# Operands of the first FFN moved by 192 bytes, table loads moved to another queue and later, three more constant matmuls

## The chip, the cores and the metric

The kernel runs on one core of a Trainium2 chip. The metric is device time in microseconds (us) of one execution; the median of three runs of the kernel before is 2201.35 us (2201.22 to 2201.47). The change is judged by that time alone.

## The reference, cut to what matters

One layer of a decoder trunk over T = 272 positions (16 learned tokens ahead of 256 tokens), width 2048, all in float32:

```
h += 1/2 * SwiGLU_1(RMSNorm(h))              # first FFN, 2048 -> 5632 -> 2048, 272 positions
u  = RMSNorm(h);  z = u @ W_in               # mix: sparse attention and a gated short convolution
h += W_out(sigmoid(ga) * y_attn + sigmoid(gc) * y_conv)
h += 1/2 * SwiGLU_2(RMSNorm(h))              # second FFN, 256 positions
return h without the first 16 positions
```

`SwiGLU(x) = (silu(x @ w_gate) * (x @ w_up)) @ w_down`. All weights together are some 390 MB and each is read from HBM once.

## The kernel before, in words

**Numbers in two parts.** Each float32 value is split into a high part (`hi`, type float32r) and the rest (`lo`). A product is made of three matmuls, whi*xhi, whi*xlo and wlo*xhi (`mac`, lines 263 to 265), or, where the two parts of x lie in one 512-column operand, of two (`paired`, lines 277 and 278: whi against xhi and xlo together, wlo against xhi).

**The stream of weights.** `Stream` (line 53) takes the weights in program order. Each load of 1 MB is one DMA on SyncE's queue (SP, line 93) into one of three `raw` buffers. A load is split in pieces of 8 blocks of 128x128 by ScalarE (`whi`, line 108) and VectorE (`wlo`, line 109), three pieces ahead of use. TensorE takes block after block; each is the stationary operand of two or three matmuls, and the columns of the activations stream past it. `st.later(fn, lag)` and `st.early(fn, lag)` put other work behind or ahead of the split of a coming piece; `tables` is put at lag 16.

**Where operands lie.** `act` holds the normalised input of a stage: for each of 16 blocks of rows a row of `PITCH` = 320 float32 for hi and one for lo. `mid` holds the FFN's inner values in the same form. `LINE` is 64 float32, 256 bytes, so a row is five lines; in the built program both tiles begin on a multiple of 256 bytes. The first FFN writes and reads columns 0 to 271 of a row (`FIRST` = 0). The mix and the second FFN use columns 48 to 319 (`LATER` = 48, that is 192 bytes behind the start of a line), so that the 256 tokens proper begin on a line. In the second FFN a row of `mid` is 256 columns, all used.

**The stages.** `start_tiles` runs the first four products of the first FFN side by side while loads still arrive (PSUM tiles `start`). Then come gate and up products (`pg`, `pu`, 16 blocks deep), the down products (`pd`, 22 blocks deep), twice over; then the mix, whose first five products (`pkv`, three matmuls a block, 272 columns, `act` from column 48) have the first FFN's very shape; then the second FFN with paired matmuls. The norm's factor is applied behind the product, so that a stage can begin before the sum of squares is known; one small matmul (`norm`, line 348) adds that sum up across partitions.

**The beginning.** TensorE first multiplies a constant tile by itself nine times (`WARM`, line 259) while nothing has arrived. The first loads of weights and of `h` alternate on SP's queue; a first block of `h` and 16 columns of `small` go out on ScalarE's. The other tables (the rest of `small`, `ident`, `rope`, `cbias`) go out on GpSimd's queue (POOL, lines 236 to 239); GpSimd has nothing to wait for, so they leave at once although their place in the program is lag 16. Their first readers: the second gain in `small` at the end of the first FFN, the rest in the mix.

Of the kernel before, what the change touches and what calls it, by code (L numbers as in the profile page):

```python
# [17 lines left out]
KD = D // P  # L18
# [4 lines left out]
META = 16  # L23
# [23 lines left out]
RAW_BUFS = 3  # L47
SPLIT_BUFS = 4
AHEAD = 3
WARM = 9  # L50

LINE = 64
PITCH = 5 * LINE
FIRST, LATER = 0, LINE - META
SUB = 1024
RAW = 2048

# [95 lines left out]
def tile_decoder_layer(  # L155
# [22 lines left out]
    nc = tc.nc  # L178
# [7 lines left out]
    st = Stream(nc, raw_pool, split_pool)  # L186
# [30 lines left out]
    small = const.tile([P, SMALL], F32, name="small")  # L217
    rope = const.tile([P, 3, ROPE], F32, name="rope")
    cbias = const.tile([P, 2, T], F32, name="cbias")
    ident = const.tile([P, P], F32, name="ident")  # L220
# [12 lines left out]
    st.load(3, [load_h(1, 2), load_h(2, 4), load_h(4, 8), load_h(8, 12), load_h(12, 16)])  # L233

    def tables():
        nc.gpsimd.dma_start(small[:, KD:], small_in[:, KD:])
        nc.gpsimd.dma_start(ident, ident_in)
        nc.gpsimd.dma_start(rope, rope_in)
        nc.gpsimd.dma_start(cbias, cbias_in)

    st.later(tables, 16)

    o = 3 * KD
    gains = [small[:, i * KD : (i + 1) * KD] for i in range(3)]
# [5 lines left out]
    def mm_tile(name="mm"):  # L250
        return psum.tile([P, 512], F32, name=name, tag="mm")
# [5 lines left out]
    warm = mm_tile("warm")  # L257
    for _ in range(WARM):
        nc.tensor.matmul(warm[:, :P], ones, ones, start=True, stop=True)
# [7 lines left out]
    def fmajor(ps, xhi, xlo, n):  # L267

        for k in range(n):
            whi, wlo = st.next()  # L270
            mac(ps, whi, wlo, xhi(k), xlo(k), k == 0, k == n - 1)

    def paired(ps, x, n):

        for k in range(n):
            whi, wlo = st.next()
            nc.tensor.matmul(ps.rearrange("p (a t) -> p a t", a=2), whi, x(k), start=k == 0, stop=False)  # L277
            nc.tensor.matmul(ps[:, :SEQ], wlo, x(k)[:, 0, :], start=False, stop=k == n - 1)  # L278

    def joined(out, ps):  # L280
        u = tmp.tile([P, T], F32, name="u", tag="sq")[:, :SEQ]
        nc.scalar.activation(u, ps[:, SEQ:], AF.Copy)
        nc.vector.tensor_add(out, ps[:, :SEQ], u)
# [10 lines left out]
    def split_into(hi, lo, src):  # L294
        nc.scalar.activation(hi, src, AF.Copy)
        nc.vector.tensor_sub(lo, src, hi.bitcast(F32))

    def parts(at):

        return (lambda k, c0=0, c1=T: act[:, k, 0, at + c0 : at + c1]), (  # L300
            lambda k, c0=0, c1=T: act[:, k, 1, at + c0 : at + c1]
        )

    def next_act(d, gain, c0, at):

        x = h[:, d, c0:]
        g = gain[:, d : d + 1]
        hi, lo = (f(d, c0) for f in parts(at))
        nc.scalar.activation(hi, x, AF.Copy, scale=g)
        nc.vector.scalar_tensor_tensor(lo, x, g, hi.bitcast(F32), op0=ALU.mult, op1=ALU.subtract)  # L310
# [28 lines left out]
    def norm(c0, lag, ps, columns=False):  # L339

        box = {}

        def total():
            nc.vector.tensor_add(ssq[0][:, c0:], ssq[0][:, c0:], ssq[1][:, c0:])

        def across():
            row = ps[:, :T] if not columns else ps[:, 0, :T]
            nc.tensor.matmul(row[:, c0:], ones, ssq[0][:, c0:], start=True, stop=True)
            box[0] = rsqrt(R[:, c0:], row[:, c0:], (P, T - c0), 1.0 / D)
            if columns:  # L350
                for j, t0 in enumerate((0, META, META + P)):
                    nc.tensor.matmul(
                        ps[:, 1, 2 * j : 2 * j + 2], ssq[0][:, t0 : t0 + P], ones[:, :2], start=True, stop=True
                    )

        def inverse():
            box[0][1]()
            if columns:
                nc.vector.tensor_mul(R2, R, R)
                for fn in rsqrt(rcol, ps[:, 1, :6], (P, 6), 1.0 / D):  # L360
                    fn()

        st.later(total, lag)
        st.early(across, lag + 1)
        st.later(lambda: box[0][0](), lag + 1)
        st.later(inverse, lag + 2)

    def start_tiles(n, xhi, xlo):

        two = [aux_tile(f"start{i}") for i in range(2)]  # L370
        four = [two[i // 2][:, i % 2, :] for i in range(4)]
        for k in range(KD):
            for ps in four:
                whi, wlo = st.next()
                mac(ps[:, :n], whi, wlo, xhi(k), xlo(k), k == 0, k == KD - 1)
        return four

    def ffn(c0, at, done, wait, starting):
        n = T - c0
        a_hi, a_lo = parts(at)  # L380
        pitch = PITCH if n > SEQ else SEQ
        with tc.tile_pool(name=f"ffn{c0}", bufs=2, reuse_waits="tile") as fp:
            mid = fp.tile([P, FHALF, 2, pitch], F32R, name="mid", bufs=1)
            i_hi, i_lo = mid[:, :, 0, :n], mid[:, :, 1, :n]
            xhi, xlo = (lambda k: a_hi(k, c0)), (lambda k: a_lo(k, c0))
            pairs = n == SEQ

            def up(ps):
                if pairs:
                    paired(ps, lambda k: act[:, k, :, at + c0 : at + T], KD)  # L390
                else:
                    fmajor(ps[:, :n], xhi, xlo, KD)

            def down(ps, last):
                if pairs and not last:
                    paired(ps, lambda k: mid[:, k, :, :], FHALF)
                else:
                    fmajor(ps[:, :n], lambda k: i_hi[:, k, :], lambda k: i_lo[:, k, :], FHALF)

            def normed(out, ps):  # L400
                if pairs:
                    joined(out, ps)
                    nc.vector.tensor_mul(out, out, R[:, c0:])
                else:
                    nc.vector.tensor_mul(out, ps[:, :n], R[:, c0:])

            def gate(pg, box):
                box["t"] = fp.tile([P, n], F32, name="t")
                normed(box["t"], pg)

            def silu(box):
                box["s"] = fp.tile([P, n], F32, name="s")
                nc.scalar.activation(box["s"], box["t"], AF.Silu)

            def times(pu, box):
                box["v"] = fp.tile([P, n], F32, name="v")
                normed(box["v"], pu)
                nc.vector.tensor_mul(box["v"], box["v"], box["s"])

            norm(c0, wait, mm_tile("norm"))  # L420
            least = st.at + wait + 1
            for c in range(2):
                for f in range(FHALF):
                    box = {}
                    side = int(starting and c == 0 and f < 2)
                    if side:
                        if f == 0:
                            four = start_tiles(n, xhi, xlo)
                        pg, pu = four[2 * f : 2 * f + 2]
                    else:  # L430
                        pg, pu = mm_tile("pg"), mm_tile("pu")
                        up(pg)
                    st.later(lambda pg=pg, box=box: gate(pg, box), 1, least)
                    st.later(lambda box=box: silu(box), 2, least + 1)
                    if not side:
                        up(pu)
                    st.later(lambda pu=pu, box=box: times(pu, box), 1 + side, least + 1)
                    st.later(lambda f=f, box=box: split_into(i_hi[:, f, :], i_lo[:, f, :], box["v"]), 2 + side, least + 2)
                for d in range(KD):
                    pd = mm_tile("pd")  # L440
                    last = d == KD - 1 and c == 1
                    down(pd, last)
                    st.later(lambda d=d, pd=pd, last=last: add_to(h[:, d, c0:], pd, 0.5, pairs and not last))
                    if c == 1:
                        done(d)
            if not starting:
                st.flush()
# [3 lines left out]

    for u in range(AHEAD + 1):
        for d in (u,) if u < 2 else (2 * u - 2, 2 * u - 1):
            next_act(d, gains[0], 0, FIRST)
        st.split(u + 1)
    for u in range(AHEAD + 1, KD // 2 + 1):
        st.early(lambda u=u: [next_act(d, gains[0], 0, FIRST) for d in (2 * u - 2, 2 * u - 1)], u - AHEAD + 1)
    for d in range(KD):
        st.later(lambda d=d: square(d, 0), 4 + d * 7 // KD)

    def done1(d):
        st.later(lambda: (next_act(d, gains[1], 0, LATER), square(d, 0)), 2)

    ffn(0, FIRST, done1, 10, True)


    with ExitStack() as mix:
# [578 lines left out]
```

## Time and profile before

| | us |
|---|---|
| median of three runs | 2201.35 |
| the profiled execution, its own time | 2201.42 |
| its span, first to last instruction | 2199.3 |
| first FFN | from 7.26 to 806.08 of the span |
| mix | to 1461.5 |
| second FFN | to the end |

The profiled execution's time is 2.1 us above its span (2201.42 against 2199.3), and 0.07 us above the median. How to read the rows below: times in rows of the timeline are from the span's start; a row of the timeline gives start, duration, engine, line, operation and operands, and in brackets how long the engine had been idle and what ended that. The durations of matmuls overlap, since they are pipelined; the pace of TensorE is the distance from one start to the next, which is why first and last rows of a stretch are shown with the count between. In the table of stretches the count of matmuls takes in the two that reach over from the stretch ahead. "PEclk" is the granted clock of TensorE as a share of full speed, 2.4 GHz.

### The profile page before, as it was taken

Reading aid. Unit: us, or ns where it says so; the run is one execution under the profiler, and the core shown is the slowest. Engines: PE = TensorE matmul, PEld = TensorE weight load, DVE = VectorE, ACT = ScalarE, POOL = GpSimd, SP = SyncE. Lnnn points to the kernel's source line nnn. Section 1 sums busy time; section 2 is a strip of 40 time slices with the busy share of each in tenths; the row PEclk is TensorE's granted clock in tenths of the full one; section 3 lists DMA queues with packets and bytes.
Section 4 is the critical chain, followed back from the end, with each engine's and each line's share of the span. In section 5 each row is a group of like instructions: output and inputs, shape, how many; then the busy total and the mean of one; then the engine's idle time right before and its main releaser. Section 6 shows DMA issues by size and latency. Waiting matters only on the chain.

```text
span 2199.3 us, 34921 instructions
## 1 busy us (share of the span) xinstructions
PE 2188.4 (100%) x14548; PEld 2014.9 (92%) x14548; DVE 1318.3 (60%) x1848; ACT 1015.9 (46%) x1460; POOL 17.7 (1%) x30
## 2 busy tenths in 40 slices
PE   9999999999999999999999999999999999999999
PEld 8999999999999998798988888888888888888888
DVE  7555544455555555786566677676666556666654
ACT  6434433343444445564454455554444444444443
POOL 0000000000000000000000000000000000000000
PEclk9999999999999999999999999999999999999999
DMA  6544555444445445444455555545555555555553
GB/s 243 192 173 173 175 179 179 177 173 173 173 174 178 179 153 191 157 151 152 166 181 190 192 173 191 191 174 192 191 190 191 192 191 192 189 188 188 189 206 132
DMA packets 56510, 397.89 MB, mean 181 GB/s; under 512 B 6560, under 2 KB 7328, under 8 KB 8864
## 3 DMA queue, kind: packets, MB, share of 16 engines
q1 hardware_dynamic: 55296, 393.36, 50.7%
q8 instruction: 114, 1.87, 0.3%
q0 software_dynamic: 768, 2.16, 0.3%
q14 instruction: 44, 0.36, 0.0%
q10 hardware_dynamic: 288, 0.15, 0.0%
HBM read 393.54 MB, written 2.10 MB: 180 GB/s over the span
## 4 chain that ended last, share of the span: by engine, by line
PE 97%; DVE 1%; ACT 1%; DMA 1%; issue 0%; DVEq 0%; ACTq 0%
PE pu L277 7%; PE pg L277 7%; PE pd L277 7%; PE pgt L277 5%; PE pd L263 4%; PE pd L265 4%; PE pd L264 4%; PE pu L265 4%; PE pu L264 4%; PE pu L263 4%; PE pg L265 4%; PE pg L264 4%; PE pg L263 4%; PE pu L278 4%; PE pg L278 4%; PE pd L278 4%
## 5 line engine op out<-in xcount | busy, mean ns | idle before, releaser
L109 DVE TENSOR_TENSOR wlo<-raw,whi 128x1024 fp32r<-128x1024 f32 (+1 forms) x747 | 913.3, 1223 | 807.2 <-ACT whi L108 806.5
L108 ACT ACTIVATE whi<-raw 128x1024 fp32r<-128x1024 f32 (+1 forms) x747 | 789.0, 1057 | 999.3 <-issue 159.2
L277 PE MATMUL pg<-act,whi 128*128 128x512 f32 x704 | 246.3, 394 | 0.4 <-DVE act L310 0.4
L277 PE MATMUL pu<-act,whi 128*128 128x512 f32 x704 | 246.2, 394 | 0.0
L277 PE MATMUL pd<-mid,whi 128*128 128x512 f32 x682 | 236.5, 394 | 0.0
L265 PE MATMUL pd<-mid,wlo 128*128 128x272 f32 (+1 forms) x726 | 208.6, 287 | 0.0
L264 PE MATMUL pd<-mid,whi 128*128 128x272 f32 (+1 forms) x726 | 208.6, 287 | 0.0
L263 PE MATMUL pd<-mid,whi 128*128 128x272 f32 (+1 forms) x726 | 208.6, 287 | 0.0
L278 PE MATMUL pg<-act,wlo 128*128 128x256 f32 x704 | 195.1, 277 | 0.0
L278 PE MATMUL pu<-act,wlo 128*128 128x256 f32 x704 | 195.0, 277 | 0.0
L263 PE MATMUL pg<-act,whi 128*128 128x272 f32 x672 | 193.4, 288 | 0.0
L265 PE MATMUL pg<-act,wlo 128*128 128x272 f32 x672 | 193.3, 288 | 0.0
L264 PE MATMUL pg<-act,whi 128*128 128x272 f32 x672 | 193.2, 288 | 0.0
L263 PE MATMUL pu<-act,whi 128*128 128x272 f32 x672 | 193.2, 288 | 0.0
L264 PE MATMUL pu<-act,whi 128*128 128x272 f32 x672 | 193.2, 288 | 0.0
L265 PE MATMUL pu<-act,wlo 128*128 128x272 f32 x672 | 193.2, 288 | 0.0
L278 PE MATMUL pd<-mid,wlo 128*128 128x256 f32 x682 | 188.9, 277 | 0.0
L277 PE MATMUL pgt<-act,whi 128*128 128x512 f32 x512 | 182.2, 398 | 0.0
L277 PEld LDWEIGHTS pg<-act,whi 128*128 128x128 f32 x704 | 132.0, 188 | 31.4 <-DVE act L310 0.7
L277 PEld LDWEIGHTS pu<-act,whi 128*128 128x128 f32 x704 | 132.0, 188 | 30.7
L277 PEld LDWEIGHTS pd<-mid,whi 128*128 128x128 f32 x682 | 127.9, 188 | 29.7
L278 PE MATMUL pgt<-act,wlo 128*128 128x256 f32 x512 | 143.8, 281 | 0.0
(218 smaller groups left out, 4041.9 us busy)
## 6 DMA issues: line engine op xcount, KB each, us to landing
raw<-in_wgu_dram SPq DMA_DIRECT2D x175, 1024.0 KB, 4.8
raw<-in_wd_dram SPq DMA_DIRECT2D x88, 1024.0 KB, 4.8
raw<-in_wcv_dram SPq DMA_DIRECT2D x24, 1024.0 KB, 4.7
raw<-in_wgc_dram SPq DMA_DIRECT2D x24, 1024.0 KB, 4.7
raw<-in_wga_dram SPq DMA_DIRECT2D x24, 1024.0 KB, 4.7
raw<-in_wo_dram SPq DMA_DIRECT2D x16, 1024.0 KB, 4.7
raw<-in_wqi_dram SPq DMA_DIRECT2D x8, 1024.0 KB, 4.8
raw<-in_wq_dram SPq DMA_DIRECT2D x8, 1024.0 KB, 4.7
```

Source lines behind the costliest of these rows:

```text
L108: nc.scalar.activation(hi[:, :n], raw, AF.Copy)
L109: nc.vector.tensor_sub(lo[:, :n], raw, hi[:, :n].bitcast(F32))
L263: nc.tensor.matmul(ps, whi, xhi, start=first, stop=False)
L264: nc.tensor.matmul(ps, whi, xlo, start=False, stop=False)
L265: nc.tensor.matmul(ps, wlo, xhi, start=False, stop=last)
L277: nc.tensor.matmul(ps.rearrange("p (a t) -> p a t", a=2), whi, x(k), start=k == 0, stop=False)
L278: nc.tensor.matmul(ps[:, :SEQ], wlo, x(k)[:, 0, :], start=False, stop=k == n - 1)
```

## The change

Three edits. `WARM` goes from 9 to 12. The four table loads are issued by SP and not by GpSimd. The first FFN's operands in `act` lie from column 48 of a row (`LATER`), not from 0, and those in `mid` too (`pitch - n` = 320 - 272 = 48 in the first FFN, 256 - 256 = 0 in the second, which is as before).

```diff
-WARM = 9
+WARM = 12
...
-FIRST, LATER = 0, LINE - META
+LATER = LINE - META
...
     def tables():
-        nc.gpsimd.dma_start(small[:, KD:], small_in[:, KD:])
-        nc.gpsimd.dma_start(ident, ident_in)
-        nc.gpsimd.dma_start(rope, rope_in)
-        nc.gpsimd.dma_start(cbias, cbias_in)
+        nc.sync.dma_start(small[:, KD:], small_in[:, KD:])
+        nc.sync.dma_start(ident, ident_in)
+        nc.sync.dma_start(rope, rope_in)
+        nc.sync.dma_start(cbias, cbias_in)
...
-            i_hi, i_lo = mid[:, :, 0, :n], mid[:, :, 1, :n]
+            i_hi, i_lo = (mid[:, :, i, pitch - n :] for i in range(2))
...
-            next_act(d, gains[0], 0, FIRST)
+            next_act(d, gains[0], 0, LATER)
...
-        st.early(lambda u=u: [next_act(d, gains[0], 0, FIRST) for d in (2 * u - 2, 2 * u - 1)], u - AHEAD + 1)
+        st.early(lambda u=u: [next_act(d, gains[0], 0, LATER) for d in (2 * u - 2, 2 * u - 1)], u - AHEAD + 1)
...
-    ffn(0, FIRST, done1, 10, True)
+    ffn(0, LATER, done1, 10, True)
```

On SP's queue, whose loads the stream of weights lives on, the beginning of the program reads as follows (a 128x2048 load of `raw` is 1 MB, x9 means nine in a row):

```order
 L93 DMA raw<-in_wgu_dram 128x2048
 L231 DMA h<-in_h_dram 128x1088
-L93 DMA raw<-in_wgu_dram 128x2048 x41
+L93 DMA raw<-in_wgu_dram 128x2048 x9
+L236 DMA small<-in_small_dram 128x320
+L237 DMA ident<-in_ident_dram 128x128
+L238 DMA rope<-in_rope_dram 128x144
+L239 DMA cbias<-in_cbias_dram 128x544
+L93 DMA raw<-in_wgu_dram 128x2048 x32
 L93 DMA raw<-in_wd_dram 128x2048 x22
 L93 DMA raw<-in_wgu_dram 128x2048 x44
```

The four table loads now stand behind the twelfth load of 1 MB of weights, in the midst of the first FFN's gate and up products.

On GpSimd's queue the same place, right behind the constant tile `ones` that the first matmuls read:

```order
 L1041 UNCONDITIONAL_BRANCH
 L225 MEMSET ones 128x128
-L236 DMA small<-in_small_dram 128x320
-L237 DMA ident<-in_ident_dram 128x128
-L238 DMA rope<-in_rope_dram 128x144
-L239 DMA cbias<-in_cbias_dram 128x544
 L570 MEMSET hss 128x16
 L850 ISA
```

GpSimd has no load left at the beginning. On TensorE, VectorE and ScalarE the order of instructions is the same as before but for the three added matmuls.

## Rows read from the trace of the kernel before

**Rows 1.** The page: busy us of each engine, and chain by engine.

```profile
PE 2188.4 (100%) x14548; PEld 2014.9 (92%) x14548; DVE 1318.3 (60%) x1848; ACT 1015.9 (46%) x1460; POOL 17.7 (1%) x30
...
PE 97%; DVE 1%; ACT 1%; DMA 1%; issue 0%; DVEq 0%; ACTq 0%
```

**Rows 2.** Stretches, TensorE: length, busy us (matmuls), clock, DMA share, GB/s.

```profile
42.06:276.67 234.61, 234.61 (x1874) 1.00 0.49 174
276.67:409.00 132.33, 132.33 (x1058) 1.00 0.49 176
409.00:673.67 264.67, 264.67 (x2114) 1.00 0.49 175
673.67:806.08 132.41, 132.41 (x1058) 1.00 0.49 173
1099.70:1461.50 361.80, 361.80 (x2050) 1.00 0.53 186
1468.60:2073.40 604.80, 604.80 (x3491) 1.00 0.54 189
```

**Rows 3.** Timeline of TensorE: end of the first FFN, beginning of the mix.

```profile
794.06 0.28 PE L263 MATMUL pd<-mid,whi 128*128 128x272 f32 x1
...
806.08 0.29 PE L263 MATMUL pkv<-act,whi 128*128 128x272 f32 x1
...
811.88 0.29 PE L265 MATMUL pkv<-act,wlo 128*128 128x272 f32 x1
...
826.00 0.29 PE L263 MATMUL pkv<-act,whi 128*128 128x272 f32 x1
...
836.85 0.29 PE L264 MATMUL pkv<-act,whi 128*128 128x272 f32 x1
836.98 0.28 PE L265 MATMUL pkv<-act,wlo 128*128 128x272 f32 x1
```

**Rows 4.** Timeline of TensorE and ScalarE: the four products run side by side.

```profile
18.14 0.29 PE L263 MATMUL start<-act,whi 128*128 128x272 f32 x1
...
34.74 0.29 PE L265 MATMUL start<-act,wlo 128*128 128x272 f32 x1
...
34.94 1.06 ACT L108 ACTIVATE whi<-raw 128x1024 fp32r<-128x1024 f32 x1 [1.20 <-PE start L264]
```

**Rows 5.** Timeline of the first 17 us: TensorE's waits and a ScalarE split.

```profile
7.26 0.43 PE L263 MATMUL start<-act,whi 128*128 128x272 f32 x1 [2.54 <-ACT whi L108]
...
13.03 0.39 PE L265 MATMUL start<-act,wlo 128*128 128x272 f32 x1 [0.47 <-DVE wlo L109]
...
14.40 1.06 ACT L108 ACTIVATE whi<-raw 128x1024 fp32r<-128x1024 f32 x1 [1.50 <-DMA raw<-in_wgu_dram]
...
16.77 0.39 PE L265 MATMUL start<-act,wlo 128*128 128x272 f32 x1 [0.46 <-DVE wlo L109]
```

**Rows 6.** Stretches at the beginning, all engines; and the constant matmuls by tile.

```profile
4.07:7.48 3.41, 0.87 (x7) 0.68 (x6) 0.74 (x2) 1.31 (x3) 0.00 (x0) 1.00 1.02 363
7.48:10.89 3.41, 3.34 (x15) 3.01 (x15) 2.38 (x5) 1.90 (x5) 0.00 (x0) 0.50 1.04 429
...
L259 PE MATMUL warm<-ones x18: 274/421/581, 1.0 to 4.4; 128*128 128x128 f32 x18
```

**Rows 7.** DMA, first 20 us: GpSimd's queue (packets, MB); longest table load, KB, landing.

```profile
q0 software_dynamic: 192, 0.58, 7.4%
...
cbias<-in_cbias_dram POOLq DMA_DIRECT2D x1, 272.0 KB, 6.7
```

**Rows 8.** The tables' new place: SP's load, its landing, its first reader, `act` writes.

```profile
62.59 0.33 SPq L93 DMA_DIRECT2D raw<-in_wgu_dram  x1
...
DMA to landing us min/median/max: 3.9/4.9/6.4
...
75.27 1.06 ACT L108 ACTIVATE whi<-raw 128x1024 fp32r<-128x1024 f32 x1 [1.93 <-PE pg L264]
...
L309 ACT ACTIVATE act<-h,small x48: 495/506/523, 6.2 to 1465.6; 128x272 fp32r<-128x272 f32 x32, 128x256 fp32r<-128x256 f32 x16
```

## The prediction

> **What bounds the kernel now.** I read the page first: TensorE is busy for all of the span and holds 97% of the chain that ended last; VectorE and ScalarE are at 60% and 46% [rows 1]. So time goes where TensorE's pace goes, and the pace has to be read stage by stage. In the table of stretches, PE busy equals the length of each stretch and the granted clock is 1.00: there are no stalls to remove in the first FFN between 42 and 806 us. What is left is the distance between starts. The four stretches of the first FFN hold 1872 + 1056 + 2112 + 1056 = 6096 matmuls (two of each printed count reach over from the stretch ahead) in 764.0 us, 125.33 ns each, and each stretch alone gives the same: products that read `act` from column 0 and products that read `mid` from column 0 run alike [rows 2]. 272 columns at 2.4 GHz are 113.3 ns, so 12.0 ns of each start-to-start are something else.
>
> Then I looked for the same shape elsewhere. The mix begins with `pkv`: the same three matmuls, 272 columns, the same split weights, but `act` read from column 48. The last 96 `pd` starts before it take 806.08 - 794.06 = 12.02 us, 125.2 ns each. `pkv` follows without a pause and takes 5.80 us for 47 starts, 123.4 ns. After the norm's matmuls and a product of another width it is at the same pace again: from 826.00 to 836.85 and 836.98 are 88 and 89 starts, 123.3 and 123.4 ns, mean 123.33 [rows 3]. The other inputs of that pace (clock, weights, three matmuls a block) are the same, only the column at which the operand begins is another.
>
> There is more than one pace for the same operands, though. The four products at the beginning, also from column 0, need 16.60 us for 131 starts, 126.7 ns [rows 4]; and paired matmuls of one form run at 361.80 / 2048 = 176.66 ns in the mix's last part and at 604.80 / 3489 = 173.34 ns in the second FFN [rows 2]. A pace, once taken, is kept for hundreds of matmuls and is taken anew after a pause. This is the main risk below.
>
> At the very beginning TensorE waits for data: its first real matmul starts at 7.26 us, and the `wlo` pieces that it needs at 13.03 and 16.77 come from loads that had just landed (ScalarE's split at 14.40 waits for the DMA, VectorE follows ScalarE, and TensorE at 16.77 waits for VectorE) [rows 5].
>
> **The change, part by part.**
>
> *Operands at column 48.* The instructions are the same in number and order; only addresses move. If the first FFN takes the pace that `pkv` has, 6096 starts gain 125.33 - 123.33 = 2.00 ns each: 12.2 us [rows 2, 3]. The starts ahead of 42 us from 16.77 on, some 165 of them at 126.7 ns, gain 3.3 ns each: 0.5 us [rows 4]. No row has `mid` at column 48; its bounds are its own pace now (no gain on its 2112 matmuls, 4.2 us less) and `pkv`'s. I take `pkv`'s, since `mid` and `act` agree today to the hundredth of a nanosecond. The writers move as well: ScalarE writes 16 blocks of 272 columns of `act` at column 0 and 16 at column 48, and all 48 of its writes lie within 495 to 523 ns [rows 8], so nothing moves there. Can the stream of weights feed the faster pace? A block of 64 KB per 3 x 123.33 = 370 ns is what the second FFN already does in 2 x 173.34 = 347 ns, with DMA share 0.54 [rows 2]. So nothing takes TensorE's place as the bound.
>
> A rule speaks against this term. The Trainium skill (TensorE: Matmul & The Clock Gate, section "Back-to-back issue gap") gives the distance of warm matmuls as N/2.4 + 2.5 ns, with no place for the address: an estimate by that page of 115.8 ns for 272 columns at either place, and so no gain from the shift. The trace disagrees with it twice: 125.33 at column 0 and 123.33 at column 48, and the two differ [rows 2, 3]. By that page the sum would lose its 12.7 us; it is the first rival.
>
> *Tables off GpSimd's queue.* All of GpSimd's 0.58 MB in the first 20 us are tables, and today they move beside the first weights; the longest lands 6.7 us after its issue [rows 7]. The DMA engines are full in both stretches there (share 1.02 and 1.04, 363 and 429 GB/s [rows 6]), and the landing that ends TensorE's last early wait lies behind them. At 429 GB/s, 0.58 MB are 1.35 us; I move the landing at 14.40, and the restart at 16.77, forward by that, to 15.4. Bounds: 0.5 us, if the order of issue rather than bytes holds part of it back, and 1.6 us at 363 GB/s. TensorE must be at the restart by then: the `wlo` for 13.03 moves to 11.7, from there 24 matmuls at 125 ns end by 15.0 even if it comes 0.3 us late. The early splits begin at the same landing and move with it, and by 34.94 us ScalarE waits 1.20 us for TensorE and no longer the other way round [rows 4]; so 1.35 us is kept.
>
> *Tables on SP's queue.* Four issues, at the 0.33 us of a weight load's issue 1.3 us of SP, and 1.35 us of transfer, ahead of the load at 62.59 us, the thirteenth of the stream. Queued behind them is the weight load issued at 62.59; it lands some 4.9 us later (6.4 at the most in the first FFN) and is first read at 75.27 [rows 8]. That is 7.8 us of cover for a delay of 1.3 + 1.35 = 2.7 us, so cost nothing; without the cover it would be 2.7 us once. The tables' readers come hundreds of us later. GpSimd's queue only loses work.
>
> *Three more constant matmuls.* Each runs as two in the trace; 18 starts lie in 3.4 us, so six more take 1.2 us at most [rows 6] and end at about 6 us, while the first real matmul waits for data until 7.26, or some 0.3 us sooner now. Cost nothing. The clock: in the stretch from 4.07 to 7.48, with TensorE busy for 0.87 us, the row says 1.00, and the next stretch 0.50, that is 1.2 GHz [rows 6]. Should the added matmuls keep it at 2.4 GHz, some 15 matmuls come 0.1 us sooner each, 1.5 us, and the waits at 11.7 and 15.4 take it back, since they end with landings. Gain 0; bounds 0 and 0.3 us, what TensorE may be late at 11.7.
>
> *Sum*, against the profiled execution's own 2201.42 us: 12.2 + 0.5 + 1.35 = 14.05 less, 2187.4; the median of the runs stands 0.07 lower, 2187.3.
>
> **The rivals.**
>
> *The column does nothing by itself*: `pkv`'s pace belongs to the mix, and the first FFN stays at 125.33 as the page's rule on addresses would have it. Then only the beginning gains: 2201.4 - 1.35 = 2200.1. Against it stands that `pd` and `pkv` follow each other without a pause and the first 48 starts of `pkv` already have the other pace [rows 3]. 0.10.
>
> *Slower: the first FFN takes a worse pace.* At its restart behind the early waits or the norm it settles at 126.7 ns, as the same code did between 18 and 35 us [rows 4], and keeps it. 6096 x 1.35 = 8.2 us more, less 1.35: 2208.3. It decides from a mean of 125.6 ns on, where the early gain is used up. For it: two paces are seen at column 0. Against: at column 48 all stretches of `pkv` with full-width weights show one. 0.07.
>
> *A later stage settles otherwise*, because all of it comes at another moment. The second FFN at the mix's 176.66 would pay 3.3 ns on some 4190 paired matmuls (3489 in the stretch, 700 behind it), 13.9 us: 2201.2. 0.07. The mix's last part at the second FFN's 173.34 would gain 2048 x 3.3 = 6.8: 2180.5. 0.06. Against both: the three runs lie within 0.25 us, so a stage's pace doesn't hang on chance of that size.
>
> *Only `act` gains*, `mid` stays at 125.33: 14.05 - 4.2 = 9.8 less, 2191.6. 0.06.
>
> **How the numbers follow.** My forecast, 2187.3 (2186.5 to 2188.2 by the early bounds), has 0.64. What a measurement of this kernel tells from no change is about 0.2%, 4.4 us. Faster: forecast, `act` alone, the mix's gain, 0.76. Same: column nothing and the second FFN's loss, 0.17. Slower: 0.07. For the range the forecast, the mix's gain and `act` alone hold 0.76, too little, so it reaches to 2200.5 for the first rival: 2180 to 2200.5 holds 0.86.
>
> **What would show it.** Right: in the stretches of the first FFN starts 123.3 ns apart with `act` and with `mid` alike, its 48 starts taking 5.92 us in place of 6.02; the restart of 16.77 near 15.4; `pkv` and all behind it at today's pace, 14 us sooner. Wrong: 125.3 or more in the first FFN (column or pace), a `pd` pace apart from `pg`'s, the last part of the mix or the second FFN at another pace, or a first-FFN split that waits for a `raw` load near 75 us.

## The result, and the profile after

| | before | after |
|---|---|---|
| median, us | 2201.28 (2201.19 to 2201.47, 4 runs) | 2186.12 (2185.66 to 2186.42, 4 runs) |
| profiled execution, its own time | 2201.42 | 2185.66 |
| its span | 2199.3 | 2183.9 |

The ratio is 0.9931, with a 95% interval from 0.9914 to 0.9948: 15.2 us less by the medians. The forecast was 2187.3, 14.05 us less. In later repetitions some runs of the kernel before lie 8 or 14 us higher and some of the changed kernel 14; profiles further down show stages at a slower pace that would cost this much.

TensorE is still busy for the whole span (the page of the changed kernel, busy us of each engine):

```profile
PE 2175.9 (100%) x14554; PEld 2002.7 (92%) x14554; DVE 1317.1 (60%) x1848; ACT 1015.4 (46%) x1460; POOL 15.4 (1%) x26
```

The next rows show TensorE in the changed kernel by stretches, as [rows 2] do for the kernel before: four of the first FFN, the last part of the mix, a part of the second FFN. Each gives the length, busy us, matmuls (two or three of them reach over from the stretch ahead), clock, DMA share and GB/s.

```profile
39.14:270.02 230.88, 230.88 (x1875) 1.00 0.51 180
270.02:400.26 130.24, 130.24 (x1059) 1.00 0.51 179
400.26:660.74 260.48, 260.48 (x2115) 1.00 0.51 178
660.74:790.98 130.24, 130.24 (x1059) 1.00 0.50 176
1084.58:1446.39 361.81, 361.81 (x2050) 1.00 0.53 187
1459.20:1692.16 232.96, 232.96 (x1346) 1.00 0.54 188
```

230.88 us for 1872 matmuls, 130.24 for 1056, 260.48 for 2112: 123.33 ns in each, for products that read `act` and products that read `mid`. The first FFN's 6096 matmuls take 751.84 us where they took 764.02 [rows 2]. The last part of the mix (361.81 us for 2048) and the second FFN (232.96 for 1344, 173.33 ns) are what they were. At the beginning, by the timeline of the changed kernel (start, duration, engine, line, operation, idle time before it and what ended that):

```profile
6.82 0.40 PE L263 MATMUL start<-act,whi 128*128 128x272 f32 x1 [0.34 <-ACT whi L108]
...
11.97 1.06 ACT L108 ACTIVATE whi<-raw 128x1024 fp32r<-128x1024 f32 x1 [1.51 <-DMA raw<-in_wgu_dram]
...
14.35 0.40 PE L265 MATMUL start<-act,wlo 128*128 128x272 f32 x1 [0.33 <-DVE wlo L109]
...
35.61 0.73 PE L348 MATMUL norm<-ssq,ones 128*128 128x272 f32 x2 [0.51 <-DVE ssq L344]
```

They answer to [rows 5] and to this row of the kernel before:

```profile
38.49 0.73 PE L348 MATMUL norm<-ssq,ones 128*128 128x272 f32 x2 [0.42 <-DVE ssq L344]
```

The split that waits for the load begins at 11.97 and not at 14.40, TensorE restarts at 14.35 and not at 16.77, and the norm's matmul starts at 35.61 and not at 38.49. So the 15.76 us between the two profiled executions are: 2.92 ahead of the stretches (they begin at 39.14, not 42.06), 12.18 in the first FFN, 0.3 from there to the end of the span (1393.2 us before, 1392.9 after), and 0.36 outside the span (2.12 and 1.76).

### The profile page after: what moved, and what is told of

Read it like the earlier page. It is cut to its first block, busy times and chain, and to the rows that moved or that the text cites. A ratio compares the mean times of both kernels' runs of the same rounds, so it can differ in the third digit from the quotient of the medians.

```text
span 2183.9 us, 34927 instructions
## 1 busy us (share of the span) xinstructions
PE 2175.9 (100%) x14554; PEld 2002.7 (92%) x14554; DVE 1317.1 (60%) x1848; ACT 1015.4 (46%) x1460; POOL 15.4 (1%) x26
## 4 chain that ended last, share of the span: by engine, by line
PE 96%; DVE 2%; ACT 1%; DMA 1%; issue 0%; ACTq 0%; DVEq 0%
PE pu L277 7%; PE pg L277 7%; PE pd L277 7%; PE pgt L277 6%; PE pd L264 4%; PE pd L263 4%; PE pd L265 4%; PE pu L263 4%; PE pu L265 4%; PE pu L264 4%; PE pg L263 4%; PE pg L265 4%; PE pg L264 4%; PE pu L278 4%; PE pg L278 4%; PE pd L278 4%
## 5 line engine op out<-in xcount | busy, mean ns | idle before, releaser
L108 ACT ACTIVATE whi<-raw 128x1024 fp32r<-128x1024 f32 (+1 forms) x747 | 788.5, 1056 | 985.8 <-issue 159.9
```

What stands on the lines that cost most here:

```text
L108: nc.scalar.activation(hi[:, :n], raw, AF.Copy)
```

## Experiments: which part brings what

**The columns alone.** The kernel before with one constant and the slice of `mid` changed:

```diff
-FIRST, LATER = 0, LINE - META
+FIRST, LATER = LINE - META, LINE - META
...
-            i_hi, i_lo = mid[:, :, 0, :n], mid[:, :, 1, :n]
+            i_hi, i_lo = (mid[:, :, i, pitch - n :] for i in range(2))
```

> The kernel before with one part of the change alone: the first FFN's operands in act and mid lie from column 48. If the column sets the pace: 123.3 ns from start to start in all of the first FFN, 12.2 us less there and 0.5 us less ahead of it, about 2188.6 us, with the restart near 16.8 us where it is before. If the pace came with the earlier beginning of the changed kernel and not with the column: 125.3 ns, about 2201.3 us.

Measured: 2188.67 us median (2188.33 to 2188.9, 4 runs), ratio 0.9943 (0.9928 to 0.9957). Its stretches of the first FFN, first gate and up part and first down part:

```profile
41.20:272.07 230.87, 230.87 (x1874) 1.00 0.51 177
272.07:402.31 130.24, 130.24 (x1058) 1.00 0.51 178
```

The same 123.33 ns without the other two edits, so the earlier beginning has no part in the pace, and the column brings 12.7 us of the 15.2 (against the kernel before in the same session, 2201.39).

**Only `act` moved**, `mid` from column 0:

```diff
-FIRST, LATER = 0, LINE - META
+FIRST, LATER = LINE - META, LINE - META
```

> The kernel before with act from column 48 and mid from column 0 as before. If each operand's own column sets the pace of its matmuls: gate and up products at 123.3 ns, down products at 125.3 ns, 3984 x 2.0 = 8.0 us and 0.5 us ahead of them less, about 2192.8 us. If a pace once taken is kept whatever the operand: down products at 123.3 ns too, about 2188.6 us.

Measured: 2193.3 us in one run. Its four stretches of the first FFN, in turn `act`, `mid`, `act`, `mid`:

```profile
41.75:272.63 230.88, 230.88 (x1874) 1.00 0.51 177
272.63:405.00 132.37, 132.37 (x1059) 1.00 0.50 176
405.00:665.48 260.48, 260.48 (x2114) 1.00 0.51 178
665.48:797.84 132.36, 132.36 (x1058) 1.00 0.50 173
```

123.33 ns where `act` is read, 132.37 / 1056 = 125.35 where `mid` is. The stages follow one another without a pause, so a pace isn't simply kept: each operand's own column decides, and both halves of the edit are needed. That is the first answer of the forecast.

**The tables alone**, on SP's queue:

```diff
-        nc.gpsimd.dma_start(small[:, KD:], small_in[:, KD:])
+        nc.sync.dma_start(small[:, KD:], small_in[:, KD:])
...
-        nc.gpsimd.dma_start(cbias, cbias_in)
+        nc.sync.dma_start(cbias, cbias_in)
```

> The kernel before with one part alone: the four table loads are issued by SP. If the early landings come sooner by all that they did in the changed kernel (2.4 us at the load that ends TensorE's last early wait), about 2198.9 us; if only by the tables' 0.58 MB at 429 GB/s, 1.35 us, about 2199.9 us, and the rest of the changed kernel's early gain belongs to another part. The first FFN stays at 125.3 ns by the column theory; if a shift of the beginning moves the pace, it shows here as another pace.

Measured: ten runs, eight at 2198.97 to 2200.07, two at 2207.29 and 2212.13; ratio 0.9993 (0.9975 to 1.0012). By the interval that can't be told from no change, so the gain is read from the trace. The profiled run is that of 2207.29. Its early split, two rows of the four products at the beginning with 90 starts between them, and its first FFN:

```profile
12.51 1.06 ACT L108 ACTIVATE whi<-raw 128x1024 fp32r<-128x1024 f32 x1 [1.51 <-DMA raw<-in_wgu_dram]
```

```profile
19.72 0.29 PE L264 MATMUL start<-act,whi 128*128 128x272 f32 x1
...
31.00 0.29 PE L264 MATMUL start<-act,whi 128*128 128x272 f32 x1
```

```profile
40.37:277.49 237.12, 237.12 (x1875) 1.00 0.50 175
277.49:411.25 133.76, 133.76 (x1059) 1.00 0.50 174
```

The landing comes 1.9 us sooner. But here the first FFN runs at 237.12 / 1872 = 126.67 ns, all the way through `act` and `mid`. That is the pace of the four products at the beginning of the kernel before [rows 4]; in this run those four take 11.28 us for 90 starts, 125.3 ns. So in either kernel the pace of the first FFN is another than that of the products ahead of it, the one time better and the other time worse. 6096 times 1.33 ns are 8.1 us; 2207.29 lies 7.2 to 8.3 us above the eight others. No profile shows one of the eight, nor the run of 2212.13. If the eight ran at the pace of before, the tables bring 1.3 to 2.4 us; both figures of the forecast, 2198.9 and 2199.9, are met by four runs each, so the time doesn't decide between them. What is shown is that two paces exist at column 0 with not an instruction changed.

The two groups of four go with the mean clock that was listed for each run: 2198.97 to 2199.34 at 0.999, 2200.00 to 2200.07 at 1.000. Why the runs listed with the higher clock are the slower ones is open; the next experiment shows that a listed 1.00 doesn't exclude half speed.

**Twelve constant matmuls alone:**

```diff
-WARM = 9
+WARM = 12
```

> The kernel before with one part alone: twelve constant matmuls. By my working nothing, 2201.3 us within 0.3, since TensorE's early waits end with landings whatever its clock. By the rival that the clock, which no longer fell to half speed in the changed kernel, brought part of the early gain: up to 1.5 us less, about 2199.8 us.

Measured: 2201.51 us median of ten runs (2200.93 to 2202.15), ratio 0.999 (0.9972 to 1.0008). Nothing, as forecast. The clock was not held either: in its profile the stretch at half speed, in which 14 matmuls run at 1.2 GHz, lies later than in [rows 6].

```profile
6.31:9.72 3.41, 2.87 (x18) 1.00 1.03 413
9.72:13.14 3.42, 1.62 (x11) 1.00 1.02 427
13.14:16.55 3.41, 3.29 (x14) 0.50 1.01 425
```

TensorE had been busy for 1.62 us of the stretch ahead of the fall. Here the half speed falls behind the first waits, and the norm's matmul starts at 39.26 where it starts at 38.49 in the kernel before.

Beside late tables the three matmuls are not without effect. In all nine profiles with nine constant matmuls some 10 to 25 of the first real ones, between 7 and 13 us, start 0.227 us apart, which is 272 columns at 1.2 GHz; in the four with twelve and late tables none do. The stretch of [rows 6] that holds 15 matmuls at half speed, with the columns alone, with the tables alone and in the changed kernel:

```profile
7.48:10.89 3.41, 3.41 (x15) 1.00 1.04 426
```

```profile
7.48:10.89 3.41, 3.20 (x16) 0.57 1.04 434
```

```profile
7.48:10.89 3.41, 3.34 (x25) 1.00 1.03 432
```

The first row lists 1.00 and has the count of half speed all the same, so the listed clock alone doesn't tell. With the tables early, half speed is hidden in the kernel before, since TensorE waits for landings behind it [rows 5]. With the tables late and nine matmuls it isn't: in the profile of the tables alone TensorE waits for nothing between 7.69 us and the norm, so TensorE is the later one and not the landing. From the start of the split that waits for the load to the norm's matmul pass 24.25 us there, and 24.66 in the run with late tables on GpSimd's queue (below); with more bytes (below), at the same 125.3 ns, TensorE waited for the landing, and it is 23.90. So half speed costs these two an estimated 0.4 and 0.8 us. In the changed kernel, with its waits for landings, it is 23.64, and 23.62 to 23.63 in the three other profiles of twelve with late tables. No run has the columns and the late tables with nine, so what the three matmuls save there is this estimate.

## Experiments: why the beginning gained more than its bytes

**More bytes.** 0.56 MB more on GpSimd's queue, into tiles that are overwritten later:

```diff
     nc.gpsimd.memset(ones, 1.0)
+    for i, to in enumerate((R, R2, *ssq)):
+        nc.gpsimd.dma_start(to, h_in[:, i, :])
```

> The kernel before with 0.56 MB more on GpSimd's queue at the beginning: four blocks of h are loaded into tiles whose contents are overwritten later. If the tables' price at the last early landing (14.4 us in the kernel before) is their bytes alone, it comes at 15.7 us, 1.3 us later; if bytes on that queue cost 2.2 us per 0.58 MB, as landings of 12.0 to 12.5 us without tables say, at 16.5 us or later. Time 2202.7 or 2203.6 us, if the first FFN takes 125.3 ns.

Measured: 2202.88 us in one run, at 125.33 ns in the first FFN. The split that waits for the load:

```profile
16.15 1.06 ACT L108 ACTIVATE whi<-raw 128x1024 fp32r<-128x1024 f32 x1 [1.49 <-DMA raw<-in_wgu_dram]
```

1.75 us later than in the kernel before, between the two figures. 0.56 MB in 1.75 us are 318 GB/s, less than the 429 of the sum. It is one run, and the same split of seven kernels with early tables begins at 14.04 to 14.71 (below); against these it is 1.4 to 2.1 us later, where 429 GB/s would make it 1.3.

**Late, but on GpSimd's queue.** GpSimd first copies one column of the norm's result:

```diff
-    const.tile([P, 32], F32, name="lead")
+    lead = const.tile([P, 32], F32, name="lead")
...
     def tables():
+        nc.gpsimd.tensor_copy(lead[:, :1], R[:, :1])
         nc.gpsimd.dma_start(small[:, KD:], small_in[:, KD:])
```

> The kernel before, tables still on GpSimd's queue, but GpSimd first copies one element of R, the first FFN's norm, so that the loads go out near 41 us. If it is their moment and not their queue that costs, the landing that is at 14.4 us in the kernel before comes at 12.0 to 12.6 us as with the tables on SP, and the time is 2199 to 2200 us where the first FFN takes 125.3 ns. If it is GpSimd's queue, the gain is absent: 2201.4 us.

Measured: the split begins at 12.29, as with the tables on SP:

```profile
12.29 1.06 ACT L108 ACTIVATE whi<-raw 128x1024 fp32r<-128x1024 f32 x1 [1.51 <-DMA raw<-in_wgu_dram]
```

So it is the moment and not the queue. The time settles nothing: ten runs, seven from 2199.44 to 2201.61 and three from 2214.03 to 2215.29, ratio 1.0014 (0.999 to 1.0038). The forecast of 2199 to 2200 us was met by one of them. In the profiled run, 2200.68 us, the gain at the norm is 1.5 us, 0.6 less than at the split; TensorE waits for nothing from 7.87 us to the norm, as with the tables alone.

```profile
36.95 0.72 PE L349 MATMUL norm<-ssq,ones 128*128 128x272 f32 x2 [0.47 <-DVE ssq L345]
```

The rest of the span gives 0.4 back, all of it between the first FFN and the last part of the mix (294.06 us, in the kernel before 293.62); why is open.

What remains: without the tables early, the split began at 11.97, 12.29 and 12.51, with them at 14.40 in the kernel before. That is 1.9 to 2.4 us, not 1.35. Over all profiles here the split begins at 14.04 to 14.71 in the seven kernels with the tables early as in the kernel before (mean 14.46) and at 11.97 to 12.59 in the six without (mean 12.32): 2.1 us, and no overlap. The ends that the kernel before and the changed one don't show:

```profile
14.04 1.06 ACT L108 ACTIVATE whi<-raw 128x1024 fp32r<-128x1024 f32 x1 [1.49 <-DMA raw<-in_wgu_dram]
14.71 1.06 ACT L108 ACTIVATE whi<-raw 128x1024 fp32r<-128x1024 f32 x1 [1.50 <-DMA raw<-in_wgu_dram]
12.59 1.06 ACT L108 ACTIVATE whi<-raw 128x1024 fp32r<-128x1024 f32 x1 [1.51 <-DMA raw<-in_wgu_dram]
```

(the columns alone; columns 16 and 32; the changed kernel with one more constant matmul). The order of issue is not it: the load is issued at 4.94 to 5.47 us with the tables early and at 4.94 to 5.39 without. Counted in bytes, more had to move than the tables. The stretch up to the split, in the kernel before and in the changed one:

```profile
0.00:14.40 14.40, 10.32 (x55) 0.88 0.85 313
```

```profile
0.00:11.97 11.97, 10.43 (x59) 1.00 0.81 302
```

313 GB/s for 14.40 us are 4.51 MB, 302 for 11.97 are 3.61: 0.90 MB less had moved by the time of the landing, of which the tables are 0.58. The other 0.3 MB are bytes of other loads, some 0.75 us at 429 GB/s; why they had moved ahead of this landing only with the tables early is open. A smaller part may be the engines' rate: in the stretch from 4.07 to 7.48, 392 GB/s in the changed kernel where it was 363 [rows 6],

```profile
4.07:7.48 3.41, 2.93 (x14) 2.41 (x12) 1.18 (x3) 1.75 (x4) 0.00 (x0) 1.00 1.03 392
```

29 GB/s over 3.41 us, 0.10 MB, 0.23 us at 429 GB/s. That part is not sure, since the rates of this stretch overlap: 334 to 376 in the seven kernels, 373 to 394 in the six.

## Experiments: which column

**Columns 16 and 32, 40 and 44, 36 and 24**, for `act` and `mid` in this order; the edit for the first pair:

```diff
-FIRST, LATER = 0, LINE - META
+FIRST, LATER = 16, LINE - META
...
-            i_hi, i_lo = mid[:, :, 0, :n], mid[:, :, 1, :n]
+            o = 32 if n > SEQ else 0
+            i_hi, i_lo = (mid[:, :, i, o : o + n] for i in range(2))
```

> The kernel before with act from column 16 (64 bytes behind a line) and mid from column 32 (128 bytes). If any start off the beginning of a line is enough, both at 123.3 ns, about 2188.6 us. If it is the end that counts (only from column 48 does an operand of 272 columns end with a line), both at 125.3 or 126.7 ns, 2201 to 2209 us. Gate and up products read the one place, down products the other, so each has its own answer.

> The kernel before with act from column 40 (160 bytes behind a line) and mid from column 44 (176 bytes), neither a multiple of 64 bytes. If the nearness to the line's end were enough, close to 123.3 ns; if the place within 64 bytes counts, a pace worse than 125.3 ns, as the mix's operands of 258 columns from column 62 have more than their columns' worth (119.0 to 124.3 ns against 107.5); no figure for that is forecast but that it lies between 123.3 and 130 ns.

> The kernel before with act from column 36 (144 bytes behind a line) and mid from column 24 (96 bytes). Columns 40, 44 and 48 took 123.3 ns, columns 16 and 32 took 126.7. If the switch is a place in the line, between columns 32 and 40, act is at one of the two and mid at 126.7 ns: 2196 to 2209 us. If it is rather that multiples of 16 columns other than 48 are bad, both are at 123.3 ns, 2188.7 us.

Measured, one run each: 2209.88, 2202.9 and 2198.93 us. The stretches of columns 16 (`act`) and 32 (`mid`):

```profile
42.40:279.52 237.12, 237.12 (x1875) 1.00 0.49 173
279.52:413.28 133.76, 133.76 (x1059) 1.00 0.50 174
```

of columns 40 and 44, and of the second FFN in the same run:

```profile
41.74:272.62 230.88, 230.88 (x1875) 1.00 0.51 177
272.62:402.86 130.24, 130.24 (x1058) 1.00 0.51 179
...
1462.05:1699.48 237.43, 237.43 (x1346) 1.00 0.52 185
```

and of columns 36, 24, 36, 24:

```profile
41.64:274.60 232.96, 232.96 (x1875) 1.00 0.50 176
274.60:406.95 132.35, 132.35 (x1058) 1.00 0.49 176
406.95:669.78 262.83, 262.83 (x2115) 1.00 0.50 176
669.78:803.54 133.76, 133.76 (x1059) 1.00 0.48 171
```

| column | ns from start to start |
|---|---|
| 0 | 125.33 or 126.67 |
| 16 | 126.67 |
| 24 | 125.33, and 126.67 in the second half |
| 32 | 126.67 |
| 36 | 124.44 |
| 40, 44 | 123.33 |
| 48 | 123.33, in every profile with it |

Column 48 isn't singular: an operand that begins at column 40, 44 or 48 of the 64 in a 256-byte line has the good pace, whether or not it ends with a line and whether or not it begins on 64 bytes. So "any start off a line", "the end of a line" and "multiples of 16" are out, and 124.44 at column 36 was in no forecast. At columns 16, 24 and 32 only the two paces of column 0 were seen, in one run each; at column 24 the pace changed from the one down stretch to the other with no pause between. All these operands touch five lines of 256 bytes, so it isn't their number. No column behind the first line was tried, so that the pattern returns with every 256 bytes is not shown. That column 40 is not as good as 48 in its time (2202.9) is another thing: there the second FFN, whose columns are untouched, took 237.43 / 1344 = 176.66 ns and not 173.33.

## Experiments: how a pace is chosen

**One constant matmul ahead of the last part of the mix**, which has 176.66 ns in all profiles so far while the second FFN has 173.33 for matmuls of the same form. In the changed kernel:

```diff
+        nc.tensor.matmul(mm_tile("again")[:, :P], ones, ones, start=True, stop=True)
         for branch, merge in ((conv_out, conv_merge), (attn_out, attn_merge)):
```

> The changed kernel with one constant matmul of 128 columns ahead of the last part of the mix. If a pace is taken anew after any break of the pattern, that part may take the second FFN's 173.3 ns in place of 176.7: 2048 x 3.3 ns = 6.8 us less, about 2179.5 us. If the pace there belongs to the operands and not to the break, 2186.3 us.

Measured: 2186.27 us median (2185.99 to 2186.53, 4 runs), and that part as before:

```profile
1085.36:1447.26 361.90, 361.90 (x2052) 1.00 0.53 186
```

In four runs a break in the pattern alone changes nothing.

**A pause**, with a matmul that waits for VectorE:

```diff
+        nc.vector.tensor_copy(ssq[1][:, META:], pb[:, :SEQ])
+        nc.tensor.matmul(mm_tile("again")[:, :SEQ], ones, ssq[1][:, META:], start=True, stop=True)
         for branch, merge in ((conv_out, conv_merge), (attn_out, attn_merge)):
```

> The changed kernel with a pause of TensorE ahead of the last part of the mix: VectorE copies the last pb, and a constant matmul of 256 columns waits for the copy, as the norm's matmul waits ahead of the second FFN. If the pause lets the paired matmuls take the second FFN's 173.3 ns: 6.8 us less and some 1.2 us for the pause, about 2180.6 us. If that part keeps 176.6 ns as it did behind one constant matmul without a wait, about 2187.4 us, slower by the pause.

Measured, seven runs: 2180.52 and 2180.61; 2187.45, 2187.6 and 2187.6; 2194.38 and 2195.01. Ratio to before 0.9931 (0.9905 to 0.9957), the same as without the pause. The profiled run is that of 2180.61:

```profile
1086.15:1441.33 355.18, 355.18 (x2051) 1.00 0.54 189
1454.14:1687.11 232.97, 232.97 (x1347) 1.00 0.54 188
```

The part of the mix now runs at 355.18 / 2048 = 173.43 ns, the first products behind the pause included. That is the forecast 2180.6. The wait that the row of the added matmul shows is the pause:

```profile
1085.80 0.70 PE L911 MATMUL again<-ssq,ones 128*128 128x256 f32 x2 [0.71 <-DVE ssq L910]
```

The 2187.5 are the other answer of the forecast, the part at 176.66. The 2194.4 to 2195.0 are 13.8 to 14.5 us above the best, the price of a second FFN at 176.66; no profile shows one of these two runs, so that reading is by the sum. A pause lets the pace be taken anew, and which one comes differs from run to run of one program: times with that part at 173.4 ns appear only here, in four of seven runs by this reading, and in none of the twenty of the changed kernel without a pause (with and without the one matmul). The matmul added here is also wider than the one before (256 columns, not 128); the two weren't tried apart.

**The changed kernel again**, for its spread:

> The changed kernel once more, for the spread of its times. By the finding that a stage takes its pace anew at a pause, most runs at 2185.7 to 2186.5 us and a few near 2200 us, where the second FFN takes 176.6 ns (13.9 us more), as some runs of the kernel before are at 2214 to 2215 us; none near 2194 us, which would be the first FFN at 126.7 ns less the early gain, since column 48 has shown one pace only. If the shift of the beginning had removed the second FFN's choice too, all lie within 1 us.

Measured, twelve runs: eight from 2185.92 to 2186.33, four from 2199.63 to 2199.99. None near 2194. The kernel before beside it, seventeen runs: ten from 2200.83 to 2201.64, two at 2209.3, five from 2214.72 to 2215.39. By their times the same two paces of the second FFN are in both kernels, 13.7 and 13.9 us apart in the means, and the first FFN's slow pace, 8.1 us, is in two runs of the kernel before and in none of the changed one. No profile of either kernel shows such a run; the prices are those of the profiles of columns 40 and 44 (second FFN) and of the tables alone (first). Ratio 0.9934 (0.9908 to 0.9959).

## Why the prediction was right, point by point

- **Pace times count.** The term of 12.2 us came out at 12.18, and its evidence, one stage of the same form at the other column, was the right one: the columns alone bring 12.7 us with what lies ahead, against 12.2 + 0.5. That `mid` gains too was taken on their equal paces; `act` alone gave some 8 us and left `mid` at 125.35 ns, and with both moved `mid` is at 123.33.
- **The rule of the Trainium skill.** The Trainium skill (TensorE: Matmul & The Clock Gate, section "Back-to-back issue gap") gives N/2.4 + 2.5 ns for an isolated matmul; for a stream of weight loads and matmuls it says that both set the spacing, and that the formula counts too much at many columns. This kernel is such a stream, with 14548 of each [rows 1], so the prediction took for its rule what the section doesn't state of it. The 123.33 ns measured lie above the formula's 115.8 all the same. With nothing but the column changed the distance went from 125.33 to 123.33 ns, so no figure by the number of columns alone can give both, and the first rival is out.
- **The term that was mis-sized** is the tables' 1.35 us, with 0.5 to 1.6 as bounds. The landing moved by 2.4 us in the changed kernel and 1.9 and 2.1 in two others, outside the bounds. The step that failed is "At 429 GB/s, 0.58 MB are 1.35 us": by the landing 0.90 MB less had moved and not 0.58, and in the one run with bytes added they came at 318 GB/s. The restart came at 14.35 and not near 15.4. All that lies ahead of the stretches brought 2.92 us where 1.85 were forecast. With 0.36 us outside the span and 0.3 behind the first FFN, for which no term stood in the sum, that is the miss of 1.7 us between the profiled executions (15.76 against 14.05); the profiled one is the fastest of the four, and by the medians the miss is 1.2 us.
- **Tables on SP's queue** cost nothing, as argued. By the timeline of SP's queue in the changed kernel, the load behind them is issued at 59.38, some 3 us sooner than the 62.59 of [rows 8], as all of this stage comes sooner:

```profile
55.77 0.42 SPq L236 DMA_DIRECT2D small<-in_small_dram  x1
...
57.56 0.45 SPq L239 DMA_DIRECT2D cbias<-in_cbias_dram  x1
59.38 12.17 SPq L93 DMA_DIRECT2D raw<-in_wgu_dram  x3
```

  The longest load of the first FFN takes 6.9 us to land where it took 6.4 [rows 8], and TensorE doesn't wait: it is busy for all of the stretch from 39.14 to 270.02.
- **The added matmuls** cost nothing, and by themselves they brought nothing, as argued. The reason given, that the waits "take it back, since they end with landings", holds with the tables early. With them late the landing came sooner than forecast, and in two kernels with nine matmuls TensorE was later than the landing, by an estimated 0.4 and 0.8 us; the bound was 0.3. In the changed kernel TensorE is at full speed and the landing's 2.4 us are kept.
- **A step that failed without showing in the median**: "the three runs lie within 0.25 us, so a stage's pace doesn't hang on chance of that size". It does. By their times seven of seventeen runs of the kernel before had one stage at another pace, and four of twelve of the changed kernel. The share differs by session: none of 4, 4 of 19, none of 7, 1 of 16, 7 of 17 for the kernel before. That none of the result's four runs was one of these is luck by the share of four in twelve. The rival of the second FFN at 176.66 is real, but belongs to runs and not to the change; that of the first FFN at 126.7 was seen at columns 0, 16, 24 and 32 and in no run at column 48.

## What to carry to other kernels

Where matmuls run without stalls, divide a stage's length by its count, and look in the same trace for a stage of the same form whose operands lie elsewhere: two nanoseconds of difference times some thousand matmuls is a gain that costs no instruction. Read several runs before calling a pace a property of a stage, since one program can have two. A part of a change that brings nothing by itself can still be needed beside another, as the three matmuls are here beside the late tables. And loads that nobody needs early should leave late: here they cost a landing that was waited for 2.1 us on the mean, where their own bytes at the engines' rate are 1.35.

## What the runs showed of the hardware that I had not expected

- For 272 float32r columns, three matmuls a block, the distance of starts took one of four values, 123.33, 124.44, 125.33 or 126.67 ns (296 to 304 cycles at 2.4 GHz), kept for a thousand matmuls and more. The column at which the moving operand begins in a 256-byte line decides: 40, 44 and 48 gave the best; at column 0 one of two others comes, by the run. Why is open.
- Paired matmuls of 512 and 256 columns have 173.33 or 176.66 ns on the mean. A wait of TensorE of 0.71 us ahead of a stage let the pace change between them from run to run; one more matmul without a wait did not, in four runs. Why is open.
- A listed clock of 1.00 doesn't show that TensorE ran at 2.4 GHz: with the columns alone the stretch from 7.48 to 10.89 us is listed at 1.00 and holds 15 matmuls, as many as at a listed 0.50 in the kernel before, where the changed kernel has 25. The distance of starts tells.
